# Rotary heads: scores with keys on the partitions, four heads side by side, row maxima computed beforehand

## The chip, the core and the metric

One core of a Trainium2 chip runs the whole program. The metric is the device time of one execution in microseconds; the kernel was run three times. A profile of one more execution gives every instruction's start and duration on each engine: TensorE (PE, with its weight loads as PEld), VectorE (DVE), ScalarE (ACT), GpSimd (POOL), and SyncE (SP), which issues the DMAs.

## What is computed

Two layers of an encoder, applied to a sequence of 2048 tokens and to one of 256 tokens with the same weights, D = 1024. The part that matters is in the first layer: eight rotary heads in two groups of four, each group with one key and value head of 64 channels.

```python
qa = apply_rope(rms_norm(qa.reshape(B, S, A_KV_HEADS, A_GROUPS, HEAD_DIM), qn_a), ...)
ka = apply_rope(rms_norm(ka.reshape(B, S, A_KV_HEADS, HEAD_DIM), kn_a), ...)
s_a = jnp.einsum('bqkgd,bskd->bkgqs', qa_blk, ka).astype(F32) * scale
p_a = jax.nn.softmax(s_a, axis=-1).astype(va.dtype)
o_a = jnp.einsum('bkgqs,bskd->bqkgd', p_a, va)
...
y = jnp.concatenate([o_a * jax.nn.silu(ga), o_b * jax.nn.silu(gb)], axis=-1)
return y @ w_out
```

Beside them stand four differential heads (two softmaxes each, with a distance bias), then an output projection, a gated embedding, and a second layer with a pooling mixer. All is float32. A product that needs float32 accuracy is made of parts: a value is split into a high part in TensorE's one-pass format (F32R) and the rest, and the products of the parts are added up in PSUM.

## The kernel before

Stages follow one another: norm and projections of the rotary heads (`BLOCKS` of 256 tokens, two tiles of 128 each, L265 on); attention of the rotary heads (`att_a`, L434) with the projections of the differential heads (`proj_b`, L513) as filler; attention of the differential heads (`att_b`, L603) with `proj_early` (L809: half of the output projection, the embeddings' projections, a fold of the pooling weights) as filler; then the rest of the fillers, the gate of the embedding, the pooling mixer and its output. The order within a stage is written as generators whose steps carry a nominal TensorE time. `drive` (L819) takes steps of the filler until they amount to a ratio of the main steps' time: 0.59 in `att_a` as long as `proj_b` lasts, then 0.1, and 0.34 in `att_b`. `paced` (L400) mixes the second half of one unit with the first half of the next. A scheduler then places the instructions on each engine's queue, in this order as far as their inputs are ready; each engine's queue runs in its order.

A unit of `att_a` is one tile of 128 queries, one group and one pair of heads; there are 64 with S = 2048 keys and 8 with 256. Its first half (`first`, L436, through `softmax`, L370) makes the scores of each head with the queries on the partitions: for each 512 keys two matmuls into a bank of tag `a` (L377, L378; q twice on the partitions as weights, `kA` with the high part of k in partitions 0 to 63 and the low part in the others as moving side). VectorE copies them negated into the tile `s` of 128x2048 and keeps the minimum (L442), ScalarE takes the exponential of 1024 columns at a time with the row's maximum as bias and sums the row (L389), and GpSimd inverts the sum (L448, L450) and scales `s` (L452). The second half (`second`, L457, through `chunks`, L349) transposes the probabilities on TensorE, four transposes of 128x128 for two heads and two chunks of 128 keys into a bank of tag `t` (`p_split`, L339), ScalarE copies the high part `ph` out of the bank (L343), VectorE makes the low part `pl` from the bank and `ph` (L347), and two matmuls per chunk with v as weights add to a bank of tag `o` (L470, L471; 256 columns, two heads side by side). At the end the two halves of the partitions are added (L477 to L483), GpSimd multiplies by the gate (L484) and splits the result (L121, L122), and it is stored to `yT_d`. The ends are put into `pend` and emitted among the next unit's steps. The last unit's second half (`tail`) runs beside the first unit of `att_b`.

The nine blocks of `proj_b` run twice, once for each half of the columns. One block has 96 matmuls of 256 columns (gate and v), then for each of two tiles 24 of 512 columns (q and k), a copy, a square, a sum by VectorE (L584), the inverse root by GpSimd (L109, L112), a multiplication by VectorE (L586), one by GpSimd (L587), four transposes (L591) and a split.

In `att_b` GpSimd subtracts one probability tile from another (L643). PSUM has three banks of tag `a`, three of `t`, one of `o` and one of `f` (the fillers').

## Time and profile before

| | us |
|---|---|
| median of three runs | 3475.4 (3472.97 to 3479.99) |
| span of the profiled execution | 3470.0 |
| TensorE busy | 3408.2 (98%) |
| VectorE busy | 1936.7 (56%) |
| ScalarE busy | 1671.8 (48%) |
| GpSimd busy | 1662.0 (48%) |
| share of the DMA engines, main queue | 40.4% |

The span is the time from the first to the last instruction of the execution that was profiled; the times are of other executions and include what lies around it. Busy times of TensorE count overlapping matmuls once, and their ends are modelled, so the distance between the starts of two matmuls tells more than the duration of one.

### The profile page before, as it was taken

To read this page: it belongs to the slowest core of one execution; us is meant where nothing else is said; L and a number is where in the kernel's file an instruction comes from. 1 tells how busy PE (TensorE), PEld (TensorE's weight loads), DVE (VectorE), ACT (ScalarE), POOL (GpSimd) and SP (SyncE) were. 2 spreads that over 40 slices of the span, in tenths; PEclk is the share of its full clock that TensorE was granted. 3 is DMA by queue.
4 is the path that set the end of the run, shared out by engine and by line. 5 is a ranking of instruction groups with operands and counts; after the bars stand their busy time and mean duration, and the time that the engine had idled before them with its cause. 6 is when DMAs were issued, how large, how long until landed. Compare 5 with 4: busy or idle time off the path is not lost.

```text
span 3470.0 us, 60660 instructions
## 1 busy us (share of the span) xinstructions
PE 3408.2 (98%) x21942; PEld 3043.7 (88%) x21942; DVE 1936.7 (56%) x4314; ACT 1671.8 (48%) x3108; POOL 1662.0 (48%) x2013
## 2 busy tenths in 40 slices
PE   9999999999999999999999899999999999999999
PEld 8998999998899988888888788887889999988887
DVE  4336666677666677658778787763434222342222
ACT  4235666666666666546677676751324111221111
POOL 5664545454645455337777687841113455420000
PEclk9999999999999999999999999999999999999999
DMA  7444323234423224653443525268534122353332
GB/s 250 158 141 135 112 77 109 79 109 125 141 82 98 91 77 127 190 180 108 122 125 114 149 91 149 87 196 267 186 133 157 62 72 70 99 164 115 112 113 73
DMA packets 459635, 437.76 MB, mean 126 GB/s; under 512 B 33992, under 2 KB 400584, under 8 KB 458312
## 3 DMA queue, kind: packets, MB, share of 16 engines
q1 hardware_dynamic: 459336, 433.88, 40.4%
q8 instruction: 174, 2.85, 0.3%
q14 instruction: 125, 1.02, 0.1%
HBM read 269.15 MB, written 164.63 MB: 125 GB/s over the span
## 4 chain that ended last, share of the span: by engine, by line
PE 91%; DMA 4%; DVE 2%; ACT 1%; issue 1%; POOL 0%; SPq 0%; DVEq 0%; ACTq 0%; POOLq 0%
PE pf L177 10%; PE pf L179 10%; PE pf L178 10%; PE pt L339 9%; PE pa L377 6%; PE pa L378 6%; PE po L177 6%; PE po L179 6%; PE po L178 6%; PE pa L178 4%; PE pa L177 4%; PE pa L179 4%; PE po L471 3%; PE po L470 3%; PE pt L195 2%; DMA v<-vl_d 1%
## 5 line engine op out<-in xcount | busy, mean ns | idle before, releaser
L389 ACT ACTIVATE s<-s,mx 128x1024 f32<-128x1024 f32 x512 | 585.6, 1147 | 137.3 <-DVE s L442 63.4
L347 DVE TENSOR_TENSOR pl<-pt,ph 128x512 fp32r<-128x512 f32 x780 | 522.4, 686 | 195.0 <-ACT ph L343 188.1
L343 ACT CAST ph<-pt 128x512 fp32r<-128x512 f32 x780 | 438.7, 584 | 276.3 <-PE pt L339 113.5
L339 PE MATMUL pt<-ident,s 128*128 128x128 f32 x3120 | 465.3, 273 | 4.5 <-DVE pl L347 1.9
L339 PEld LDWEIGHTS pt<-ident,s 128*128 128x128 f32 x3120 | 369.7, 141 | 52.4 <-DVE pl L347 4.6
L109 POOL TENSOR_SCALAR rstd<-ss 128x1 f32<-128x1 f32 x72 | 16.0, 222 | 656.4 <-ACT xn L184 654.8
L623 DVE CUSTOM_DVE_ANT_0 s<-pa,dist,mx 128x512 f32<-128x512 f32 x384 | 286.7, 747 | 70.5 <-PE pa L378 55.8
L643 POOL TENSOR_TENSOR s<-s 128x1024 f32<-128x1024 f32 (+1 forms) x136 | 313.0, 2318 | 0.2
L452 POOL TENSOR_SCALAR s<-s,rs 128x1024 f32<-128x1024 f32 (+1 forms) x272 | 298.6, 1110 | 12.1
L442 DVE TENSOR_SCALAR_CACHE_REDUCE s<-pa,mx 128x512 f32<-128x512 f32 x384 | 286.0, 745 | 23.2 <-PE pa L378 13.9
L470 PE MATMUL po<-ph,vA 128*128 128x256 f32 x1040 | 281.2, 292 | 1.1 <-ACT ph L343 1.1
L471 PE MATMUL po<-pl,vA 128*128 128x256 f32 x1040 | 279.5, 295 | 1.1 <-DVE pl L347 1.1
L177 PE MATMUL pf<-xh,wh 128*128 128x256 f32 x944 | 265.6, 281 | 1.7 <-DMA xh<-xTh_d 1.7
L178 PE MATMUL pf<-xl,wh 128*128 128x256 f32 x944 | 266.3, 282 | 0.5 <-DMA xl<-xTl_d 0.5
L179 PE MATMUL pf<-xh,wl 128*128 128x256 f32 x944 | 265.8, 282 | 0.7 <-DVE wl L131 0.7
L377 PE MATMUL pa<-kk,q 128*128 128x512 f32 (+1 forms) x528 | 220.8, 419 | 12.8 <-DMA kk<-kTl_d 11.5
L377 PE MATMUL pa<-kA,q 128*128 128x512 f32 (+1 forms) x528 | 222.8, 422 | 3.9 <-DVE s L442 3.7
L884 DVE TENSOR_TENSOR sg<-pp,sg 128x512 f32<-128x512 f32 x72 | 50.3, 698 | 285.3 <-ACT sg L883 280.0
L378 PE MATMUL pa<-kA,q 128*128 128x512 f32 (+1 forms) x528 | 207.0, 392 | 0.0
L378 PE MATMUL pa<-kk,q 128*128 128x512 f32 (+1 forms) x528 | 206.9, 392 | 0.0
L470 PEld LDWEIGHTS po<-ph,vA 128*128 128x128 f32 x1040 | 196.8, 189 | 11.3 <-ACT ph L343 1.7
L471 PEld LDWEIGHTS po<-pl,vA 128*128 128x128 f32 x1040 | 196.7, 189 | 7.5 <-DVE pl L347 3.0
(232 smaller groups left out, 9701.0 us busy)
## 6 DMA issues: line engine op xcount, KB each, us to landing
xr<-h_d SPq DMA_DIRECT2D x54, 512.0 KB, 3.3
q<-qTh_d SPq DMA_DIRECT2D x144, 128.0 KB, 2.9
q<-qTl_d SPq DMA_DIRECT2D x144, 128.0 KB, 3.0
xh<-xTh_d SPq DMA_DIRECT2D x18, 1024.0 KB, 5.5
xl<-xTl_d SPq DMA_DIRECT2D x18, 1024.0 KB, 7.9
h_d<-xr SPq DMA_DIRECT2D x72, 256.0 KB, 4.0
pp_d<-xr SPq DMA_DIRECT2D x72, 256.0 KB, 2.1
pp<-pp_d SPq DMA_DIRECT2D x36, 512.0 KB, 3.8
```

The source lines that it names most:

```text
L177: pe.matmul(out, lhsT=lhs[0], rhs=rhs[0], start=first, stop=False)
L178: pe.matmul(out, lhsT=lhs[0], rhs=rhs[1], start=False, stop=False)
L179: pe.matmul(out, lhsT=lhs[1], rhs=rhs[0], start=False, stop=last)
L339: pe.transpose(pt[:, (c * 2 + i) * P : (c * 2 + i + 1) * P], s[:, (c0 + c) * P : (c0 + c + 1) * P], ident)
L343: ac.copy(ph, pt)
L347: ve.tensor_tensor(out=pl, in0=pt, in1=ph.bitcast(F32), op=ALU.subtract)
L377: pe.matmul(ps, lhsT=q1, rhs=k[:, i * 512 : i * 512 + w], start=True, stop=False)
L378: pe.matmul(ps, lhsT=q2, rhs=k[:, i * 512 : i * 512 + w], start=False, stop=True)
L389: ac.activation(s[:, c], s[:, c], AF.Exp, bias=bias, scale=-1.0, accum_out=sums[i])
L470: pe.matmul(ov[0][:, 0:256], lhsT=v, rhs=ph[:, c], start=c0 + c == 0, stop=False)
L471: pe.matmul(ov[0][:, 0:256], lhsT=v, rhs=pl[:, c], start=False, stop=c0 + c == nk - 1)
L643: po.tensor_tensor(out=sc[0][:, k], in0=sc[0][:, k], in1=sc[1][:, k], op=ALU.subtract)
```

## The change

Only the rotary heads change, with what is laid out for them. A unit is now a tile of 128 queries and a whole group of four heads (32 with 2048 keys, four with 256). Three things are done in another way.

- The scores have the keys on the partitions: the weights are 128 keys, the moving side is q of four heads side by side, 512 columns. k lies in two tiles: `k1` with the high part in partitions 0 to 63 and ones in two further rows, `k2` with the low part over the high part. q lies in `q1` (high part, and two rows for the negated maximum in two parts) and `q2` (high part over low part). `load_qa` loads both and clears the two rows.
- The maximum of a row is found beforehand (`shift`): scores of the high parts alone with the queries on the partitions, 16 matmuls of 512 columns, a maximum by VectorE of each, one over all, its two parts by GpSimd, four transposes, and a copy of the two rows into `q1`. The scores then come out with the maximum taken off.
- The probabilities come out of the exponential with the keys on the partitions and are not transposed (`heads`): ScalarE takes the exponential twice, once as `ph`, once as `p`; VectorE makes `pl` = `p` - `ph`; GpSimd adds `p` to `acc`, chunk by chunk; products of 512 columns. At the end `acc` is split, a product with a selector of ones sums it over the partitions and spreads the sums, and the result is multiplied by their reciprocals.

The tiles `qr`, `kd`, `qh`, `ql` of the first stage have one buffer in place of two; the last unit of `att_a` runs ahead of `att_b`, whose first keys are loaded before, and the score tiles of `att_b` are one pool of eight.

```diff
+    def load_qa(g, tq):
+        q1 = qA.tile([P, 512], F32R, tag="q1", name="q1", bufs=2)
+        q2 = qA.tile([P, 512], F32R, tag="q2", name="q2", bufs=2)
+        po.memset(q1[64:66].bitcast(F32), 0.0)
+        for t, half, d in ((q1, 0, 0), (q2, 0, 0), (q2, 64, 1)):
+            sy.dma_start(t[half : half + 64].rearrange("p (h t) -> p h t", t=P).bitcast(F32),
+                         qT_d[d][g * 256 : g * 256 + 256, tq : tq + P].rearrange("(h d) t -> d h t", d=HD))
+        return q1, q2
...
+                k1 = k1p.tile([P, 2, T], F32R, name="k1")
+                ve.memset(k1[64:66].bitcast(F32), 1.0)
+                sy.dma_start(k1[0:64, :, 0:S0].bitcast(F32), k2[64:128, :, 0:S0].bitcast(F32))
...
-                qr = p1q.tile([P, 640], F32, tag="qr", name="qr")
+                qr = p1q.tile([P, 640], F32, tag="qr", name="qr", bufs=1)
...
+        def shift(t0, S, q):
+            n = (S + 511) // 512
+            mx = small.tile([P, 4, 4], F32, tag="mx4", name="mx4")
+            for h in range(4):
+                for i in range(n):
+                    w = min(512, S - i * 512)
+                    ps = pa()[:, :w]
+                    pe.matmul(ps, lhsT=q[0][0:66, h * P : (h + 1) * P], rhs=k1[0:66, q[2], t0 + i * 512 : t0 + i * 512 + w],
+                              start=True, stop=True)
+                    ve.tensor_reduce(out=mx[:, h, i : i + 1], in_=ps, axis=AX.X, op=ALU.max)
+                    if h * n + i < 4 * n - 1:
+                        yield
+            mn = small.tile([P, 4], F32, tag="mn", name="mn")
+            ve.tensor_reduce(out=mn, in_=mx[:, :, :n], axis=AX.X, op=ALU.max, negate=True)
+            po.tensor_scalar(out=mm[:, :, 64].bitcast(F32R), in0=mn, scalar1=1.0, scalar2=1.0, op0=ALU.mult, op1=ALU.mult)
+            po.tensor_tensor(out=mm[:, :, 65].bitcast(F32R), in0=mn, in1=mm[:, :, 64], op=ALU.subtract)
+            pt = pa()
+            for h in range(4):
+                pe.transpose(pt[0:66, h * P : (h + 1) * P], mm[:, h], ident)
+            ac.copy(q[0][64:66], pt[64:66])
...
+            def products(c, ph, pl):
+                pe.matmul(ov[0], lhsT=v, rhs=ph, start=c == 0, stop=False)
+                pe.matmul(ov[0], lhsT=v, rhs=pl, start=False, stop=c == nk - 1)
+
+            for c in range(nk):
+                ks = slice(t0 + c * P, t0 + (c + 1) * P)
+                ps = pt_()
+                pe.matmul(ps, lhsT=k1[0:66, g, ks], rhs=q[0][0:66], start=True, stop=False)
+                pe.matmul(ps, lhsT=k2[:, g, ks], rhs=q[1], start=False, stop=True)
+                ph = at.tile([P, 512], F32R, tag="ph", name="ph", bufs=4)
+                pl = at.tile([P, 512], F32R, tag="pl", name="pl", bufs=4)
+                p = at.tile([P, 512], F32, tag="p", name="p", bufs=3)
+                ac.activation(ph, ps, AF.Exp)
+                ac.activation(p, ps, AF.Exp)
+                ve.tensor_tensor(out=pl, in0=p, in1=ph.bitcast(F32), op=ALU.subtract)
+                if c == 1:
+                    po.tensor_tensor(out=acc, in0=before, in1=p, op=ALU.add)
+                elif c > 1:
+                    po.tensor_tensor(out=acc, in0=acc, in1=p, op=ALU.add)
+                before = p
...
+            split_po(acc, ah, al)
+
+            def rest1():
+                pr = pa()[:, 0:256]
+                n = 0
+                for u in range(2):
+                    for x in (ah, al):
+                        pe.matmul(pr, lhsT=sel[:, u], rhs=x[:, u * 256 : u * 256 + 256], start=n == 0, stop=n == 3)
+                        n += 1
+                rc = at.tile([P, 256], F32, tag="rc", name="rc", bufs=1)
+                ve.reciprocal(rc, pr)
+                gf = gt.rearrange("p h t -> p (h t)")
+                po.tensor_tensor(out=yt, in0=yt, in1=gf, op=ALU.mult)
+                po.tensor_tensor(out=yt, in0=yt, in1=rc, op=ALU.mult)
...
+                split_po(yt, yh, yl)
...
+                yield from paced(heads(*prev) if prev else None, shift(t0, S, q),
+                                 (n if prev is None else max(2, prev[3] // P), 4 * ((S + 511) // 512)), 19.5 * S / S0)
...
+        yield -1.0
+        for _ in heads(*prev):
+            yield 19.5 / 16
```

## Rows read from the trace of the kernel before

**Rows 1.** The page: busy us by engine (share, instructions); granted TensorE clock by slice.
```profile
PE 3408.2 (98%) x21942; PEld 3043.7 (88%) x21942; DVE 1936.7 (56%) x4314; ACT 1671.8 (48%) x3108; POOL 1662.0 (48%) x2013
...
PEclk9999999999999999999999999999999999999999
```
**Rows 2.** Busy time by stretch: length, PE, PEld, DVE, ACT, POOL, clock, DMA share.
```profile
292.00:1531.00 1239.00, 1224.51 (x8278) 1103.00 (x8277) 850.85 (x1938) 788.39 (x1444) 608.52 (x877) 1.00 0.38 113
1531.00:2290.00 759.00, 731.36 (x4621) 639.59 (x4621) 597.66 (x1509) 516.73 (x972) 581.24 (x573) 1.00 0.43 126
```
**Rows 3.** TensorE in order of time: start us, duration us, line, tiles, shape.
```profile
1104.61 0.28 PE L470 MATMUL po<-ph,vA 128*128 128x256 f32 x1
1104.73 0.28 PE L471 MATMUL po<-pl,vA 128*128 128x256 f32 x1
1104.86 1.04 PE L339 MATMUL pt<-ident,s 128*128 128x128 f32 x8
1105.65 0.48 PE L377 MATMUL pa<-kA,q 128*128 128x512 f32 x1
1105.96 0.40 PE L378 MATMUL pa<-kA,q 128*128 128x512 f32 x1
1106.20 0.40 PE L377 MATMUL pa<-kA,q 128*128 128x512 f32 x1
1106.43 0.39 PE L378 MATMUL pa<-kA,q 128*128 128x512 f32 x1
```
**Rows 4.** Groups by line, 292 to 1531 us, TensorE: count | busy us, mean ns | idle before.
```profile
L339 PE MATMUL pt<-ident,s 128*128 128x128 f32 x2084 | 307.9, 273 | 2.8 <-DVE pl L347 1.9 <-POOL s L452 0.7
L470 PE MATMUL po<-ph,vA 128*128 128x256 f32 x1040 | 281.2, 292 | 1.1 <-ACT ph L343 1.1
```
**Rows 5.** Groups by line, whole span: a ScalarE and a VectorE instruction of 512 columns.
```profile
L549 ACT ACTIVATE gs<-pf 128x512 f32<-128x512 f32 x18 | 10.8, 598 | 14.0 <-PE pf L179 13.9
...
L584 DVE TENSOR_REDUCE qss<-sq 128x8 f32<-128x512 f32 x36 | 24.5, 682 | 21.8 <-ACT sq L582 21.5
```
**Rows 6.** Groups by line, whole span, GpSimd, shapes kept apart.
```profile
L643 POOL TENSOR_TENSOR s<-s 128x1024 f32<-128x1024 f32 x128 | 307.2, 2417 | 0.0
...
L112 POOL TENSOR_TENSOR rstd<-rstd,mhalf 128x8 f32<-128x8 f32 x36 | 59.6, 1657 | 2.7
L587 POOL TENSOR_TENSOR qn<-qn,gains 128x512 f32<-128x512 f32 x36 | 46.4, 1289 | 43.5 <-DVE qn L586 31.4 <-PE pt L339 9.2 <-DMA st<-in_w_out_ab_dram 2.1
...
L122 POOL TENSOR_TENSOR yl<-mixd,yh 128x512 fp32r<-128x512 f32 x28 | 36.9, 1318 | 0.3
...
L122 POOL TENSOR_TENSOR yl<-yg,yh 128x256 fp32r<-128x256 f32 x36 | 27.3, 757 | 1.4
...
L121 POOL TENSOR_SCALAR yh<-mixd 128x512 fp32r<-128x512 f32 x28 | 18.6, 663 | 55.5 <-DVE z L1044 28.3 <-DVE z L1047 13.5 <-issue 7.2
...
L121 POOL TENSOR_SCALAR yh<-yg 128x256 fp32r<-128x256 f32 x36 | 15.6, 433 | 29.9 <-DVE yg L682 24.3 <-issue 5.4
...
L109 POOL TENSOR_SCALAR rstd<-qss 128x8 f32<-128x8 f32 x36 | 7.5, 209 | 52.6 <-DVE qss L584 51.6
```
**Rows 7.** VectorE and GpSimd in order of time, three places: start us, duration us, instruction.
```profile
693.53 1.12 POOL L452 TENSOR_SCALAR s<-s,rs 128x1024 f32<-128x1024 f32 x1
694.40 0.69 DVE L347 TENSOR_TENSOR pl<-pt,ph 128x512 fp32r<-128x512 f32 x1
...
809.50 1.67 POOL L452 TENSOR_SCALAR s<-s,rs 128x1024 f32<-128x1024 f32 x1
809.57 0.68 DVE L586 TENSOR_TENSOR qn<-qn,rstd 128x512 f32<-128x512 f32 x1
...
791.73 1.61 DVE L131 SCALAR_TENSOR_TENSOR wl<-st,gmix,wh 128x512 fp32r<-128x512 f32 x1
792.78 1.55 POOL L452 TENSOR_SCALAR s<-s,rs 128x1024 f32<-128x1024 f32 x1
```
**Rows 8.** DMA issues: count, KB each, median us to landing.
```profile
q<-qTh_d SPq DMA_DIRECT2D x144, 128.0 KB, 2.9
```

More of the change, by code (lines that the diff above doesn't have):

```diff
@@ new lines, in heads @@
+        def heads(g, tq, t0, S, q):
+            nk = S // P
+            gt = at.tile([P, 2, P], F32, tag="gt", name="gt")
+            r0 = g * 256
+            for u in range(2):
+                sy.dma_start(gt[u * 64 : u * 64 + 64],
+                             gT_d[r0 + u * P : r0 + u * P + P, tq : tq + P].rearrange("(h d) t -> d h t", d=HD))
+            ov, todo = [], []
+            acc = at.tile([P, 512], F32, tag="acc", name="acc")
+            before = None
+            def products(c, ph, pl):
@@ L466, in products @@
                 if not ov:
                     ov.append(po_())
-                for c in range(2):
-                    v = vA[:, t0 // P + c0 + c, g].rearrange("p r d -> p (r d)")
-                    pe.matmul(ov[0][:, 0:256], lhsT=v, rhs=ph[:, c], start=c0 + c == 0, stop=False)
-                    pe.matmul(ov[0][:, 0:256], lhsT=v, rhs=pl[:, c], start=False, stop=c0 + c == nk - 1)
-            yield from chunks(prs, nk, products, pend)
-            o = ov[0]
-            ot = at.tile([P, P], F32, tag="ot", name="ot", bufs=1)
@@ new lines, in heads @@
+            while pend:
+                pend.pop(0)()
+            for x in todo:
+                products(*x)
+            o = ov[0]
+            ot = at.tile([P, 256], F32, tag="ot", name="ot", bufs=1)
+            ac.copy(ot[0:64], o[64:128, 0:256])
+            ac.copy(ot[64:128], o[0:64, 256:512])
+            yt = at.tile([P, 256], F32, tag="yt", name="yt")
+            ve.tensor_tensor(out=yt[0:64], in0=o[0:64, 0:256], in1=ot[0:64], op=ALU.add)
+            ve.tensor_tensor(out=yt[64:128], in0=o[64:128, 256:512], in1=ot[64:128], op=ALU.add)
@@ L608, in att_b, with keys @@
         ac.activation(dist, dist, AF.Abs)
+        def keys(h):
+            km = []
+            for m in range(2):
+                k = kvb.tile([P, T], F32R, tag="kk", name="kk", bufs=NKK)
+                r0 = h * P + m * HD
+                for half in range(2):
+                    sy.dma_start(k[half * 64 : half * 64 + 64].bitcast(F32), kT_d[half][r0 : r0 + HD, :])
+                km.append(k)
+            return km
+        km = keys(0)
+        yield 0.0
         def first(h, t0, S, q0, km, q):
@@ L618, in first @@
                 for m in range(2):
[L619 to L620 removed]
+                    s = sB.tile([P, S0], F32, tag="s", name="s")
                     def evac(c, w, ps, before, now, s=s, off=off):
@@ L694, in att_b @@
         for h in range(4):
-            km = []
-            for m in range(2):
-                k = kvb.tile([P, T], F32R, tag="kk", name="kk", bufs=NKK)
-                r0 = h * P + m * HD
-                for half in range(2):
-                    sy.dma_start(k[half * 64 : half * 64 + 64].bitcast(F32), kT_d[half][r0 : r0 + HD, :])
-                km.append(k)
+            if h:
+                km = keys(h)
             v = None
@@ L706, in att_b @@
                     n = max(2, S // 256)
-                    got = yield from paced(second(*prev) if prev else tail[0], first(h, t0, S, q0, km, q), (n, 2 * n), 15.6 * S / S0)
-                    if prev is None:
-                        yield -1.0
+                    got = yield from paced(second(*prev) if prev else None, first(h, t0, S, q0, km, q), (n, 2 * n), 15.6 * S / S0)
                     if v is None:
@@ L908, in trunk_kernel @@
     keep.close()
-    sS_.close()
     xr = loaded(0), loaded(P)
```

120 lines of the change are left out of this document (51 added, 69 removed).

## The prediction

> **What bounds the kernel now.** I read the page first. The busy line gives TensorE (PE) 98% of the span and no other engine above 56%; the line of granted clock stands at full speed in all forty slices [rows 1]. So TensorE is the bound, and a change pays by the matmul time that it takes away, as long as TensorE is kept fed. The table by stage sharpens that: in the stretch of the rotary heads, 292 to 1531 us, TensorE is idle for 14.5 of 1239 us (98.8% busy); VectorE (DVE) is at 69%, ScalarE (ACT) at 64%, GpSimd (POOL) at 49%. In the stretch of the differential heads, where VectorE reaches 79% and GpSimd 77%, TensorE falls to 96.4% [rows 2]. The reader should keep that pair: as the helpers fill up, TensorE loses.
>
> Next the price of a matmul. Durations overlap, so I take the distance between starts in the order of time: 0.12 us for 256 columns, 0.235 for 512 (0.24 and 0.23), and for eight transposes 0.79, after which the next matmul of 512 columns needs 0.31, 0.075 more than otherwise: (0.79 + 0.075) / 8 = 0.108 a transpose [rows 3].
>
> **What TensorE gains.** The rotary heads have 36 units now (tile of 128 queries, group of four heads): 32 long ones with 2048 keys, four short ones. The groups by line show 2084 transposes in the stretch (2080 by the loops, the rest belong to the next heads) and 1040 products with the high part of p, as many as with the low [rows 4].
> - Transposes gone: 2080 x 0.108 = 224.6 us.
> - Products with v: 2080 of 256 columns become 1040 of 512: 249.6 less 244.4, 5.2 gained. Scores with keys as weights: 244.5 before and 244.4 after, nothing.
> - Maxima beforehand: 512 x 0.235 and 16 x 0.12: 122.2 added. Four transposes of the maxima and four selector products a unit: 144 x 0.108 and 144 x 0.12: 32.9 added.
> Net 75 us less, if nothing else changes. No row shows a matmul of 66 rows among matmuls of 128; it costs nothing extra, or at most the 0.075 of a change of form [rows 3] (a rival below).
>
> **What the helpers get.** ScalarE: 32 exponentials of 512 columns out of PSUM a unit, at 0.60 by the Silu of that shape [rows 5], 19.2 us; enough room. VectorE: 16 reductions for the maximum at 0.68, by the reduction of 512 columns [rows 5], and 16 subtractions p - ph. GpSimd: the row scaling goes, and instead it adds up p, chunk by chunk: 15 adds of 128x512 with two inputs. The two such instructions in the trace are 1.29 (512 columns) and 2.42 for 1024, so 1.21 [rows 6]; I take 1.25. At a unit's end come the split of the sum (0.66 and 1.32), two multiplications at 0.76, the split of the result (0.43 and 0.76) and two tiny ones at 0.21 [rows 6]: 5.1 us. With the adds 23.9 us a unit.
>
> The projections of the differential heads run as filler beside this: 18 blocks of 96 x 0.12 + 48 x 0.235 + 8 x 0.108 = 23.7 us of TensorE, and 36 tiles with 0.21 + 1.66 + 1.29 on GpSimd [rows 6]. The step costs in the code (19.5 a long unit, ratio 0.59, 22 a block) spread them over some 31 long units. One unit then needs 18.8 + 0.9 + 13.7 = 33.4 us of TensorE, and GpSimd 23.9 + 3.7 = 27.5. On that count TensorE stays the bound.
>
> **Why I don't believe that count.** The old subtraction read PSUM and one SBUF tile; the new one (p - ph) reads two SBUF tiles, and so does the work of GpSimd. The trace shows what that does. Beside a subtraction from PSUM, the scaling of 1024 columns takes GpSimd 1.12 us. Beside L586, a VectorE instruction with two SBUF inputs, the same scaling takes 1.67, 0.55 more. Where L131 (two SBUF inputs too, of the same 512 columns) and the scaling meet again and again, each waits for the other: 1.61 and 1.55 us [rows 7]. The two share a way into SBUF and use it in turn.
> The Trainium skill says it as a rule (SBUF — State Buffer, Who interferes with whom): a VectorE instruction with two SBUF inputs contends with a GpSimd instruction that reads SBUF, and the one that comes second is fully blocked until the first is done. By that rule each subtraction would cost GpSimd its whole 0.69 instead of the 0.55 of the row, 2.2 us a unit more, some 70 us more in all; I go by the row.
>
> So I sum the shared way, not the engines: 27.5 us of GpSimd a unit, 16 x 0.55 = 8.8 for the subtractions, 36 x 0.55 / 31 = 0.6 for L586: 36.9 us. TensorE's 33.4 is no longer the largest. Subtraction and add of a chunk wait for the same exponential, so they come at the same moment and meet. A way used in turn is not used without gaps; I give it the 96.4% that the bounding engine reaches in the fullest stage before [rows 2]: 38.3 us a unit.
>
> **The sum**, against the profiled execution (span 3470.0 us, the median of the three runs is 5.4 above it):
> - 75 us of matmul time gone.
> - 31 x (38.3 - 33.4) = 152 us in which TensorE waits for p and pl, now the last to arrive.
> - The 14.5 us that TensorE was idle in this stretch are inside that, so they come off.
> - The seam: the last unit used to run beside the first of the differential heads and now runs alone: ScalarE's 19.2 against 64 x 0.235 = 15.0 of TensorE, and the end of the chain (two exponentials, a subtraction): 7 us; between 0 and 15.
> - Nothing for the four short units beyond the counts above, nor for the first stage, whose tiles qr, kd, qh, ql lose a buffer: each block of two tiles has 96 x 0.12 = 11.5 us of gate products that don't touch them. Without that cover a block's second tile would wait for up to the 24 x 0.235 + 24 x 0.12 = 8.5 us of the first, 9 times. The copy of k1 is one transfer, issued before the last block's 2 x 8.5 + 11.5 us of matmuls and needed after them; it costs at most its own landing, once.
> - Nothing for the new wait of TensorE: the transposes of the maxima need a reduction (0.68, then a small one), then two tiny GpSimd instructions, and every later matmul is queued behind them on TensorE. The order before puts ready matmuls ahead of such chains (transposes waited 2.8 us in 1239) [rows 4]. With the cover gone, 0.68 + 3 x 0.21 = 1.3 us, 32 times: 42 us.
> -75 + 152 - 14.5 + 7 = +69.5: 3539.5, with the 5.4 **3545 us**. The add at 1.21 or 1.29 moves it by 19 us either way, a way without any gap (36.9 a unit) gives 3501, one used to 93% 3588: own range 3495 to 3590.
>
> **The rivals.**
> - *Subtraction and add miss each other* (the other side). VectorE has a reduction between most subtractions, and GpSimd is idle for part of a unit; if the reads fall into those gaps, TensorE stays the bound at 98.8%: 33.8 us a unit, -75 + 12 - 14.5 + 7 = -70: 3405 us. It decides at 33.4 + 82.5 / 31 = 36.1 us a unit, below which the change pays. For it: in the stage before, VectorE has 31% to spare; against it: both wait for the same event.
> - *VectorE becomes the bound*: each subtraction waits for a whole add, and the reductions stand behind it in VectorE's queue: 16 x (1.25 + 0.55 + 0.68) = 39.7, and 126 instructions of the projections at 0.68, 2.8 a unit: 42.5 us, 3675 us.
> - *q comes late*: a unit's q1 uses the buffer of the unit before the last, which is read to that one's last score; its memset on GpSimd stands behind the last adds, and the load takes 2.9 us to land [rows 8]. All of it exposed in front of the first maximum: 32 x 2.9 = 93 us on top of the first rival, 3498. Under the forecast the other waits hide it.
> - *66 rows cost a change of form*: 0.075 at 32 places for the scores and up to 32 for the maxima, 4.8 us x 32 = 154 on top of the first rival: 3559.
> The Trainium skill has a rule beside that last one (TensorEngine Tiling (Array Packing), Key Properties): changing the tiling mode drains TensorE; its modes split at 64 rows and below, so 66 would change nothing. No row here shows it either way.
>
> **How the numbers follow.** Forecast 0.60; misses 0.25, of which 0.02 end close to no change; VectorE bound 0.07; q late or form 0.08, slower both, with 0.01 within no change. A time within 0.2% of 3475.4 (3468 to 3482, about what a measurement of this kernel can tell from no change) gets 0.05 with the forecast's own lower tail; faster 0.24; slower 0.71. The range reaches into the first rival to 3425, where half of its 0.25 lies below, and up to 3605, which leaves the VectorE case out.
>
> **What would show it.** In the changed kernel the stretch of the rotary heads should take about 38 us a long unit with TensorE busy for some 85 to 90% of it; the subtraction's mean duration should stand well above 0.69 and the add's above 1.25; TensorE's waits should name ph, pl or the exponentials' banks. If the subtraction's mean is near 0.69 and TensorE near 98%, the first rival holds. If matmul starts stand further apart than 0.235 without a wait, it is the form; if the first maximum of a unit waits for a DMA, it is q. I am wrong at the root if the new subtraction doesn't take the shared way at all.

## The result and the profile after

| | before | after |
|---|---|---|
| median, us | 3477.6 | 3706.0 |
| lowest to highest | 3472.97 to 3479.99 | 3703.70 to 3708.11 |
| span of the profiled execution | 3470.0 | 3706.3 |

The ratio is 1.066, interval 1.064 to 1.067. The forecast was 3545 us with a range up to 3605: the sign was right, the loss three times as large (228 us by the medians, 236 between the two profiled executions, against 70).

The page of the changed kernel, its busy line and its line of granted clock, beside [rows 1]:

```profile
PE 3501.0 (94%) x19622; PEld 2971.1 (80%) x19622; DVE 2223.6 (60%) x3787; ACT 1647.1 (44%) x3050; POOL 2158.0 (58%) x2065
...
PEclk9997999989889989999999999999999999999999
```

TensorE is still the busiest, at 94% instead of 98%. Its busy time has grown by 93 us although it has 2320 instructions fewer, and the clock line, which was flat, now has dents. The dents explain part of the growth; how much in the middle of the rotary heads is worked out below, in the paragraph on the clock.

The table by stretch of the changed kernel; columns as in [rows 2]. The first row is the start of the rotary heads, the second their middle, the fourth the end of the differential heads.

```profile
300.00:350.00 50.00, 41.53 (x144) 29.52 (x143) 42.43 (x63) 22.29 (x42) 22.95 (x19) 0.63 0.57 166
350.00:1640.00 1290.00, 1169.78 (x5434) 915.63 (x5434) 1048.65 (x1283) 713.19 (x1293) 1044.17 (x871) 0.92 0.28 81
1640.00:1700.00 60.00, 54.21 (x234) 43.04 (x233) 42.69 (x47) 26.53 (x47) 44.10 (x36) 0.97 0.82 228
2500.00:2550.00 50.00, 37.94 (x152) 27.26 (x152) 20.64 (x34) 22.00 (x40) 2.75 (x3) 0.83 0.70 227
```

And the same stretches of the kernel before:

```profile
292.00:350.00 58.00, 52.98 (x335) 43.90 (x334) 49.73 (x108) 43.91 (x74) 28.69 (x35) 1.00 0.57 169
350.00:1480.00 1130.00, 1120.53 (x7630) 1013.86 (x7629) 769.99 (x1763) 719.87 (x1319) 562.98 (x812) 1.00 0.37 109
1480.00:1531.00 51.00, 51.00 (x319) 45.25 (x317) 31.12 (x69) 24.61 (x52) 16.85 (x31) 1.00 0.44 136
2300.00:2350.00 50.00, 47.68 (x260) 40.59 (x260) 24.09 (x40) 13.82 (x23) 7.85 (x8) 0.97 0.73 237
```

The middle is 160 us longer. No engine fills it: TensorE 91%, VectorE 81%, GpSimd 81%, ScalarE 55%. Long units start 40.9 us apart on the mean (30 distances between the instructions that close a unit's maxima), against 38.3 forecast.

The groups by line of the stretch 300 to 1697 us (count | busy us, mean ns | idle before):

```profile
L523 POOL TENSOR_TENSOR acc<-acc,p 128x512 f32<-128x512 f32 x448 | 671.9, 1500 | 112.4 <-ACT p L518 88.5 <-PE pt L935 4.8 <-PE pt L513 0.5
...
L519 DVE TENSOR_TENSOR pl<-p,ph 128x512 fp32r<-128x512 f32 x520 | 593.9, 1161 | 61.4 <-ACT p L518 43.1 <-PE po L507 13.0 <-PE po L506 1.2
L479 DVE TENSOR_REDUCE mx<-pa 128x1 f32<-128x512 f32 (+1 forms) x528 | 342.0, 670 | 112.3 <-PE pa L477 110.9
```

And TensorE's waits in the same stretch (us in total, times, longest):

```profile
PE po L507 <- DVE pl L519: 57.2, 75, 2.9
PE pa L477 <- DVE mx L479: 16.8, 20, 1.8
PE pt L512 <- ACT p L518: 15.4, 23, 1.9
PE pa L488 <- POOL mm L485: 12.0, 12, 2.4
PE pf L664 <- POOL qn L660: 10.7, 7, 3.4
```

The subtraction (L519) takes 1.16 us instead of 0.69 [rows 7], the add (L523) 1.50 instead of 1.25 to 1.29 [rows 6], and the product with `pl` is what TensorE waits for most. The maxima's reductions stand at 0.67, as costed [rows 5].

**Where the time lies.** From here on I count, in each stretch, the matmuls by width at the prices of [rows 3] (0.12, 0.235, 0.108 a transpose; 178 tiny ones left out) and call the rest of the stretch its excess: waiting, matmuls at the lower clock, and what else TensorE is counted busy beyond these prices. Over the whole execution the matmuls come to 3393.5 us before (7232 of 512 columns, 10376 of 256, 4156 transposes) and 3318.6 after (8800, 8424, 2220). That is 74.9 less, the forecast's 75. The excess went from 76.6 to 387.8, 311 more. Each row of the table is one profiled execution, with the bounds of the stretches set by that kernel's own course.

| excess, us | first stage and start | middle of the rotary heads | their end | differential heads | end of these | rest | sum |
|---|---|---|---|---|---|---|---|
| before | 16.9 | 12.6 | 0.0 | 50.4 | 4.3 | -7.6 | 76.6 |
| before, single buffers (g1_single) | 41.4 | 13.1 | 0.0 | 48.0 | 3.7 | -4.1 | 102.1 |
| changed kernel | 45.5 | 259.5 | 8.1 | 60.8 | 22.3 | -8.4 | 387.8 |
| subtractions from PSUM (e1_psum) | 43.7 | 169.4 | 5.8 | 58.8 | 16.9 | -10.7 | 283.9 |
| without adds (e2_noadd) | 43.8 | 115.9 | 9.2 | 56.1 | 21.3 | -8.8 | 237.5 |
| without subtractions (e3_nosub) | 42.1 | 105.7 | 1.7 | 52.1 | 19.3 | -9.0 | 211.9 |
| without either (f4_neither) | 41.9 | 48.6 | 19.1 | 55.7 | 21.2 | -11.2 | 175.3 |

The other rows belong to the experiments below. (The rest is below zero because its matmuls stand at 0.23 rather than 0.235.)

### The profile page after: what moved, and what is told of

It is laid out like the page before. It is cut to its first block, busy times and chain, and to the rows that moved or that the text cites. A ratio compares the mean times of both kernels' runs of the same rounds, so it can differ in the third digit from the quotient of the medians.

```text
span 3706.3 us, 54927 instructions
## 1 busy us (share of the span) xinstructions
PE 3501.0 (94%) x19622; PEld 2971.1 (80%) x19622; DVE 2223.6 (60%) x3787; ACT 1647.1 (44%) x3050; POOL 2158.0 (58%) x2065
## 3 DMA queue, kind: packets, MB, share of 16 engines
q1 hardware_dynamic: 449688, 430.21, 38.3%
## 4 chain that ended last, share of the span: by engine, by line
PE 76%; DVE 8%; DMA 5%; POOL 5%; issue 3%; ACT 2%; SPq 0%; POOLq 0%; DVEq 0%; ACTq 0%
PE pf L178 9%; PE pf L179 9%; PE pf L180 9%; PE po L178 6%; PE po L180 6%; PE po L179 6%; PE pa L178 4%; PE pa L179 4%; PE pa L180 4%; DVE pl L519 3%; PE pa L409 3%; PE pa L410 3%; PE pt L371 3%; DVE mx L479 3%; POOL acc L523 2%
## 5 line engine op out<-in xcount | busy, mean ns | idle before, releaser
L523 POOL TENSOR_TENSOR acc<-acc,p 128x512 f32<-128x512 f32 x448 | 671.9, 1500 | 112.4 <-ACT p L518 88.5
L519 DVE TENSOR_TENSOR pl<-p,ph 128x512 fp32r<-128x512 f32 x520 | 593.9, 1161 | 61.4 <-ACT p L518 43.1
L479 DVE TENSOR_REDUCE mx<-pa 128x1 f32<-128x512 f32 (+1 forms) x528 | 342.0, 670 | 112.3 <-PE pa L477 110.9
L517 ACT ACTIVATE ph<-pt 128x512 fp32r<-128x512 f32 x520 | 312.9, 605 | 179.5 <-PE pt L513 132.8
L518 ACT ACTIVATE p<-pt 128x512 f32<-128x512 f32 x520 | 313.1, 605 | 115.5 <-POOL acc L523 68.2
L421 ACT ACTIVATE s<-s,mx 128x1024 f32<-128x1024 f32 x256 | 292.7, 1147 | 88.3 <-DVE mx L708 86.6
L507 PE MATMUL po<-pl,vA 128*128 128x512 f32 x520 | 233.1, 448 | 58.6 <-DVE pl L519 57.2
L477 PE MATMUL pa<-k,q 66*128 66x512 f32 (+1 forms) x528 | 222.7, 453 | 25.4 <-DVE mx L479 16.8
L512 PE MATMUL pt<-q,k 66*128 66x512 f32 x520 | 225.5, 434 | 16.9 <-ACT p L518 15.4
L513 PE MATMUL pt<-q,k 128*128 128x512 f32 x520 | 219.6, 422 | 0.0
```

The lines of the kernel that those rows point to most:

```text
L479: ve.tensor_reduce(out=mx[:, h, i : i + 1], in_=ps, axis=AX.X, op=ALU.max)
L507: pe.matmul(ov[0], lhsT=v, rhs=pl, start=False, stop=c == nk - 1)
L517: ac.activation(ph, ps, AF.Exp)
L518: ac.activation(p, ps, AF.Exp)
L519: ve.tensor_tensor(out=pl, in0=p, in1=ph.bitcast(F32), op=ALU.subtract)
L523: po.tensor_tensor(out=acc, in0=acc, in1=p, op=ALU.add)
```

## The experiments

The theory after the result: subtraction and add meet on the shared way, as forecast, TensorE waits, and its clock falls, which the sum left out. Rivals: the order of TensorE's queue (maxima, seams between units) makes the waits whatever the helpers take; or the helpers' load does it without any sharing. All times are medians, to be held against 3473 to 3478 for the kernel before and 3706.0 for the changed one.

**Take the meeting away.** The second exponential is written over the scores in PSUM, so that the subtraction has one SBUF input.

```diff
-                ac.activation(p, ps, AF.Exp)
-                ve.tensor_tensor(out=pl, in0=p, in1=ph.bitcast(F32), op=ALU.subtract)
+                ac.activation(ps, ps, AF.Exp)
+                ve.tensor_tensor(out=pl, in0=ps, in1=ph.bitcast(F32), op=ALU.subtract)
...
-                    po.tensor_tensor(out=acc, in0=acc, in1=p, op=ALU.add)
+                    po.tensor_tensor(out=acc, in0=acc, in1=ph.bitcast(F32), op=ALU.add)
```

> The second exponential is written over the scores in PSUM instead of into an SBUF tile, so the subtraction reads PSUM and one SBUF tile, as the kernel before did; GpSimd adds up the high parts alone (the row sums leave out the low parts). Instruction counts on every engine stay. Theory (the two-input subtraction and GpSimd's add use one way in turn; TensorE waits, and its clock falls to the lower level): the subtraction goes back from 1.16 to about 0.69 us, the add from 1.50 to about 1.27, TensorE is busy for 97% or more of the stretch of the rotary heads at a granted clock of 0.99 or more, and the time is 3400 to 3460 us. Rival (the order of TensorE's queue: transposes of the maxima and products that wait at the head of it, whatever the helpers' instructions take): the waits stay, 3620 us or more. Second rival (GpSimd's own 27 us a unit come too late even without sharing): the add goes back to 1.27 but TensorE still waits, 3550 to 3620.

Measured: 3613.4 us, ratio 1.041 (1.038 to 1.043). The groups by line, 300 to 1697 us, and then the busy time of the middle:

```profile
L522 POOL TENSOR_TENSOR acc<-acc,ph 128x512 f32<-128x512 f32 x448 | 587.1, 1311 | 205.0 <-ACT ph L516 184.2 <-PE pt L513 3.9 <-PE pf L180 0.2
L518 DVE TENSOR_TENSOR pl<-pt,ph 128x512 fp32r<-128x512 f32 x520 | 350.0, 681 | 142.1 <-ACT pt L517 136.8 <-PE pt L513 3.8
```
```profile
350.00:1550.00 1200.00, 1123.29 (x5431) 894.65 (x5429) 822.88 (x1281) 705.71 (x1290) 888.03 (x871) 0.95 0.31 88
```

Both durations fell to what they are alone (all 520 subtractions under 0.70 us), and 93 us came back. So the meeting is real and costs 93 us. (The variant also holds the scores' bank until the subtraction; where there are no adds, that made no difference, 3560 against 3556 us below.) But the kernel stays 140 us above the one before, with TensorE at a clock of 0.95 in the middle, and the theory had asked for 3400 to 3460. The time lies in the range of the second rival (3550 to 3620: the add is back at its own duration, and TensorE waits all the same). The next runs ask whether it is GpSimd's load alone, as that rival says.

**Take the work away.** The first run leaves out fourteen of the fifteen adds of a unit (the one left reads one tile), the second leaves out the subtraction and uses the high part twice, the third leaves out both.

```diff
 e2_noadd
-                    po.tensor_tensor(out=acc, in0=before, in1=p, op=ALU.add)
-                elif c > 1:
-                    po.tensor_tensor(out=acc, in0=acc, in1=p, op=ALU.add)
+                    po.tensor_scalar(out=acc, in0=before, scalar1=1.0, scalar2=1.0, op0=ALU.mult, op1=ALU.add)
 e3_nosub
-                ve.tensor_tensor(out=pl, in0=p, in1=ph.bitcast(F32), op=ALU.subtract)
...
-                todo.append((c, ph, pl))
+                todo.append((c, ph, ph))
```

> Of the fifteen adds of a unit one is left (it reads one tile and adds a constant), so the row sums are left out of the computation; everything else stays, the two-input subtraction too. Theory: with nothing of GpSimd's beside it the subtraction is near 0.7 us and the time is 3400 to 3460 us, as where the subtraction reads PSUM. Rival (the order of TensorE's queue): 3620 us or more. Rival (the two reads of SBUF are slow by themselves, without GpSimd): the subtraction stays above 1.0 us.

> The subtraction is left out and the products read the high part twice (the low part of the probabilities is left out of the computation); both exponentials and all adds stay. Theory (sharing): the adds go to about 1.27 us, GpSimd needs 27.5 us a unit against TensorE's 33.4, and the time is 3400 to 3460 us. Rival (GpSimd's adds by themselves are the bound, the subtraction only waits along): the adds alone hold the unit, 3550 us or more.

> Both the subtractions and fourteen of fifteen adds are left out (the low parts of the probabilities and the row sums are left out of the computation), so nothing is left that could meet on the shared way within a unit. Without the subtraction alone the time was 3533 us, without the adds alone 3556. Theory A (what is left there is the helpers' load): now 3400 to 3460 us. Theory B (what is left is the seam between two units: the last products, the transposes of the maxima, the load of q and the first maxima stand one behind the other on TensorE with little ready work between them): 3490 to 3530 us, with the waits and low clock still at the seam.

Measured: 3556.4, 3533.4 and 3495.9 us (the last 1.006, 1.005 to 1.008). The first two meet none of the times that were expected: sharing alone (3400 to 3460) would have been faster, the rivals (3620 or 3550 and more) slower. The subtraction without adds, the add without subtractions, and the middle with neither:

```profile
L519 DVE TENSOR_TENSOR pl<-p,ph 128x512 fp32r<-128x512 f32 x520 | 390.0, 767 | 76.0 <-ACT p L518 59.5 <-PE po L507 15.0 <-PE pt L513 0.4
```
```profile
L521 POOL TENSOR_TENSOR acc<-acc,p 128x512 f32<-128x512 f32 x448 | 584.7, 1305 | 137.8 <-ACT p L517 117.0 <-DVE mn L483 2.5 <-DMA q<-qTh_d 1.5
```
```profile
350.00:1400.00 1050.00, 1016.34 (x5304) 854.47 (x5304) 489.23 (x753) 669.00 (x1244) 313.20 (x435) 0.99 0.33 95
...
2300.00:2350.00 50.00, 39.31 (x128) 27.23 (x127) 15.05 (x24) 14.79 (x26) 1.13 (x2) 0.74 0.71 228
```

This gives a ladder. With neither, the kernel is 23 us above the one before although 75 us of matmuls are gone. The adds alone cost 37 us more, the subtractions alone 60, both kept apart 117 (e1_psum), both together 210. So GpSimd's load, the second rival of e1_psum, is only a part of it. By the table, the steps lie in the middle stretch: 49, 106, 116, 169, 260. With neither, that stretch runs at a clock of 0.99, and most of what is left sits at the edges of the stages. Theory B of the last expectation was right in size (3490 to 3530) and largely wrong in place: the seams between units are in the middle stretch, whose excess is only 36 us above before; 63 us more lie in the other columns of the table.

**Is the subtraction's cost its two inputs?**

> The subtraction reads PSUM and one SBUF tile, and fourteen of fifteen adds are left out (row sums left out of the computation), so VectorE has its load and GpSimd next to none. With neither subtraction nor adds 3496 us, with the two-input subtraction alone 3556. If it is VectorE's load (16 x 0.68 us more a unit, and its place between scores and products) that cost the 60 us: 3540 to 3560 us. If it is the second SBUF input, slow or held up even without the adds: 3500 to 3520 us.

The edit is e1_psum and e2_noadd together. Measured: 3560.2 us (1.025, 1.023 to 1.026), the same as with two SBUF inputs (3556.4). So the second input is free in time where GpSimd has no adds to make, and 60 us are the price of the subtraction itself, by VectorE's load or by its place between scores and products; the run can't tell these two apart.

**Are the adds waited for as a whole?** Each add as two of 256 columns.

```diff
+                    for x in (slice(0, 256), slice(256, 512)):
+                        po.tensor_tensor(out=acc[:, x], in0=acc[:, x], in1=p[:, x], op=ALU.add)
```

> The changed kernel with every add done as two of 256 columns, one after the other (each about 0.72 us by the multiplications of that size, so 0.18 us more a chunk for GpSimd). If a subtraction that comes second waits for the whole instruction of GpSimd: its longest durations fall from 1.7 to 1.8 us to about 1.4 (0.69 + 0.72), its mean from 1.16 to 0.95 to 1.05, and the time to 3640 to 3700 us in spite of the longer adds. If the two share the way evenly while both run: mean and longest stay, and the time rises to 3710 to 3760 us.

Measured: 3728.5 us (1.072).

```profile
L525 POOL TENSOR_TENSOR acc<-acc,p 128x256 f32<-128x256 f32 x869 | 769.6, 912 | 55.9 <-ACT p L518 52.2
L519 DVE TENSOR_TENSOR pl<-p,ph 128x512 fp32r<-128x512 f32 x506 | 473.2, 945 | 129.6 <-ACT p L518 117.4 <-PE po L507 4.1 <-PE pf L180 1.3
```

In the changed kernel 180 of 520 subtractions took 1.35 us or more (up to 1.83) and 179 under 0.8; with halved adds 10 and 209, and the mean fell to 0.95. So a subtraction that comes second waits for the end of GpSimd's instruction, as the first answer says; the ten that are left are up to 1.80 us. But the time rose, into the range of the second answer: a chunk now costs GpSimd 2 x 0.91 = 1.82 us instead of 1.50. What shorter waits on VectorE gave was lost on GpSimd; the run doesn't say what they would be worth alone.

**Is the low clock a cause of its own?** The first score matmul of each chunk is done twice.

```diff
+                pe.matmul(ps, lhsT=k1[0:66, g, ks], rhs=q[0][0:66], start=True, stop=True)
```

> Nothing is left out; the first score matmul of every chunk is done twice, the second time over the first, which adds 16 x 0.235 = 3.8 us of TensorE work to a long unit, 122 us in all, just where TensorE is idle between chunks. Three answers. If the lower clock is what was missing in my sum (busy time 184 us above what the same matmuls take at full clock, idle 133 us as forecast), the added work keeps the clock up and the time falls or hardly rises: 3560 to 3690 us, granted clock in the stretch above 0.96. If VectorE and GpSimd set the pace at 41 us a unit and the clock only follows, nothing changes: 3690 to 3730. If TensorE is the bound at its lower clock, the added work comes on top: 3800 us or more, clock about 0.91.

Measured: 3729.2 us (1.073). 520 matmuls, 122 us at 0.235, cost 23 us. The middle stretch:

```profile
350.00:1670.00 1320.00, 1232.64 (x5923) 994.41 (x5922) 1042.00 (x1283) 724.11 (x1291) 1044.39 (x869) 0.95 0.28 81
```

In the changed kernel TensorE was idle there for 120 of 1290 us, and busy for 139 us more than its matmuls' price. Here it is idle for 87 and over price by 87 (1232.6 less 1145.2). The added work took the place of both. So in this stretch the helpers set the pace, and the second answer holds in size (3690 to 3730), though not to the letter: it said that nothing changes, and the time rose by 23 us.

**Do the maxima and the seams cost more than their matmuls?** Two runs leave out the maxima with all that belongs to them: f3_nomax starts from the changed kernel, h1_bare from the variant with neither subtractions nor adds. g3_seam, from that variant too, keeps the maxima and has a third buffer of q1, the two small instructions of the maxima on VectorE, and products three chunks behind the scores.

```diff
 f3_nomax, h1_bare
-                    pe.matmul(ps, lhsT=q[0][0:66, h * P : (h + 1) * P], rhs=k1[0:66, q[2], t0 + i * 512 : t0 + i * 512 + w],
-                              start=True, stop=True)
-                    ve.tensor_reduce(out=mx[:, h, i : i + 1], in_=ps, axis=AX.X, op=ALU.max)
...
-                ac.activation(ph, ps, AF.Exp)
+                ac.activation(ph, ps, AF.Exp, scale=0.01)
 g3_seam
-LATE_A = 2
+LATE_A = 3
...
-        q1 = qA.tile([P, 512], F32R, tag="q1", name="q1", bufs=2)
+        q1 = qA.tile([P, 512], F32R, tag="q1", name="q1", bufs=3)
...
-            po.tensor_tensor(out=mm[:, :, 65].bitcast(F32R), in0=mn, in1=mm[:, :, 64], op=ALU.subtract)
+            ve.tensor_tensor(out=mm[:, :, 65].bitcast(F32R), in0=mn, in1=mm[:, :, 64], op=ALU.subtract)
```

> The maxima are left out, with their matmuls, reductions, transposes and the copy into q (the scores are scaled down by 0.01 in the exponentials instead, so that they stay finite); subtractions and adds stay as in the changed kernel. The matmuls that go are 138 us. If the maxima cost their matmul time alone: 3568 us. If the pace is set by the shared way (36.9 us a unit, whatever the maxima do): about 3545 to 3600. If the chain of the maxima and VectorE's 16 reductions between the subtractions are what makes TensorE wait beyond my sum: 3430 to 3520.

> Subtractions, adds and the maxima with all that belongs to them are left out together (scores scaled down by 0.01 in the exponentials). Without subtractions and adds alone it was 3496 us. The matmuls of the maxima are 138 us. If the maxima cost only these: 3350 to 3365 us. If the waits that are left (20 us where the first unit's maxima run alone, 36 us at the seams) belong to the chain of the maxima: 3300 to 3335 us. If the seam costs the same without them, because products and scores of two units follow each other there: above 3350.

> The variant without subtractions and adds (3496 us; low parts and row sums left out of the computation) with the three repairs of the seam between two units: a third buffer of q1, the two small instructions of the maxima on VectorE, products three chunks behind the scores. There TensorE loses 36 us at the 32 seams, beside 44 us at the start, the ends and the first stage that these repairs don't touch. If the chain of the maxima and the load of q make the seam: 3460 to 3480 us. If it is the order of the queue whatever stands in it: 3485 to 3500.

Measured: 3585.6, 3352.5 and 3495.7 us. Without maxima, subtractions and adds the time is 143 us below that without the last two: the 138 us of matmuls and no chain worth naming. In the changed kernel even a little less came back, 120, which fits the answer that the middle's pace isn't TensorE's there (3545 to 3600). The seam's repairs gave nothing once the helpers were out of the way (3495.7 against 3495.9).

**Repairs where the helpers work.** On e1_psum: q1's third buffer (f1_q3); products three chunks behind (g2_late); the small instructions of the maxima on VectorE (i1_mm); all three (f2_all). The last but one also on the changed kernel itself (i2_mm). The edits are those of g3_seam.

> On top of the variant with the exponential in PSUM (3613 us): q1 gets a third buffer, so the load of a unit's q no longer waits for the last score of the unit before the last. If the load is part of the seam: 3570 to 3600 us, and no wait of a maximum for q is left. If the other waits of the seam cover it: 3605 to 3620.

> The variant with the exponential in PSUM (3613 us), and the products three chunks behind the scores instead of two; q and the two small instructions of the maxima as in the changed kernel. With these two changed as well it was 3573 us, with q alone 3609. If the closeness of product and subtraction is what helped: 3570 to 3585 us, and the products' wait for the subtraction falls from 25 us to under 12. If it was the maxima's way round GpSimd: 3600 us or more.

> The variant with the exponential in PSUM (3613 us) with one further change: the two small instructions of the maxima on VectorE instead of GpSimd. With q1's third buffer alone it was 3609, with later products alone 3603, with all three 3573. If the maxima's way round GpSimd is what the three-part variant gained: 3575 to 3590 us, and the transposes wait less than the 10.1 us of that variant. If the three only work together (each alone moves the wait to the next): 3600 to 3615.

> On top of that: the two small instructions of the maxima on VectorE instead of GpSimd (there they stand behind an add), and the products one chunk later (three chunks behind the scores instead of two, with five buffers of the two parts). If the seam's chain and the closeness of product and subtraction hold what is left (waits of products for the subtraction 45 us, of the transposes 13, of first maxima 44, and the low clock behind them): 3480 to 3560 us. If it is the load of VectorE: 3590 us or more.

> The changed kernel itself (3706 us) with the two small instructions of the maxima on VectorE instead of GpSimd. The transposes of the maxima waited 12.0 us for GpSimd there. If that wait and the low clock behind it are an own term: 3670 to 3695 us. If the meeting of subtraction and add sets the pace in the middle of the stretch, whatever the maxima wait for: 3698 to 3715.

Measured: 3608.5, 3603.4, 3588.0, 3573.1 (1.028, 1.027 to 1.030), and 3700.0. Against 3613.4 the first is 5 us (within the scatter of the two), the second 10, the third 25, all three 40: by the medians they add up. All three stay above the 3480 to 3560 us that were expected if the seam and the closeness of product and subtraction held all that was left. Moving the maxima's two instructions out of GpSimd's queue is the largest single gain; on the changed kernel it is worth 6 us, hardly more than the scatter, as expected if the meeting sets the pace there. How the 25 us come about isn't shown: the transposes' own wait fell only from 10.1 to 6.9 us (300 to 1600 us). How TensorE's waits move (300 to 1600 us), e1_psum first, then g2_late:

```profile
PE po L507 <- DVE pl L518: 25.4, 36, 2.3
...
PE pt L512 <- DVE pl L518: 5.5, 5, 1.9
```
```profile
PE pt L512 <- DVE pl L518: 16.4, 23, 2.7
PE po L507 <- DVE pl L518: 11.8, 12, 1.8
```

Later products wait less for the subtraction, but the next scores wait more for it, since it holds their bank. None of these variants reaches the kernel before.

**The single buffers.** The kernel before with `bufs=1` for `qr`, `kd`, `qh` and `ql`, and nothing else.

```diff
-                qr = p1q.tile([P, 640], F32, tag="qr", name="qr")
+                qr = p1q.tile([P, 640], F32, tag="qr", name="qr", bufs=1)
```

> The kernel before with one buffer instead of two for the four tiles of the first stage, and nothing else of the change. The changed kernel's first stage ends 8 to 11 us later and TensorE waits there 8.0 us, four times, for VectorE's qn, which holds the banks of the projections. If the single buffers are that: 8 to 13 us slower than before, a ratio of about 1.003. If it is the work placed beside the last block (the copy of k1, the memsets, the first loads): within 3 us.

Measured: 3494.7 us, ratio 1.0046 (1.0034 to 1.0059), 16 us, more than the 8 to 13 expected. TensorE's waits, 0 to 320 us:

```profile
PE pa L177 <- DVE qn L290: 8.0, 4, 2.9
PE pa L377 <- DVE qn L290: 5.4, 1, 5.4
```

The first row is the changed kernel's own, where the same wait is 8.0 us in four. The second comes at the start of the heads, which my expectation left out. In the table the first stage and the start have the same excess here (41.4) as in every variant of the changed kernel there (41.9 to 45.5).

## Why the prediction missed, by its steps

| term | forecast | profiled executions |
|---|---|---|
| matmuls | -75 | -74.9 |
| middle of the rotary heads (+152, -14.5) | +137.5 | +246.9 |
| seam behind the last unit | +7 | +8.1 |
| first stage and start | 0 | +28.6 |
| differential heads and their end | 0 | +28.4 |
| rest | 0 | -0.8 |
| sum | +69.5 | +236.3 |

**The matmul count held.** So did the price of nothing for matmuls of 66 rows: among those of 128 they stand 0.23 apart (the variant without subtractions, in order of time), which takes the rival of the change of form away:

```profile
735.16 0.39 PE L512 MATMUL pt<-q,k 66*128 66x512 f32 x1
735.39 0.40 PE L513 MATMUL pt<-q,k 128*128 128x512 f32 x1
735.62 0.40 PE L512 MATMUL pt<-q,k 66*128 66x512 f32 x1
```

The late q is no term either: 2.3 us of waits in the changed kernel's stretch name it, and a third buffer gave 5 on e1_psum, within the scatter. The transposes of the maxima, put at nothing because ready matmuls would cover them, waited 12.0 us in twelve places in the changed kernel; taking their two small instructions away from GpSimd gave 6 us there.

**The shared way was rightly seen and mis-priced.** Its signs all appeared: a subtraction at 1.16, adds at 1.50, waits for `pl`, TensorE 91% busy in the middle (85 to 90 had been expected). Four microseconds of the changed kernel, in order of time:

```profile
1305.07 1.54 DVE L519 TENSOR_TENSOR pl<-p,ph 128x512 fp32r<-128x512 f32 x1
1306.03 1.72 POOL L523 TENSOR_TENSOR acc<-acc,p 128x512 f32<-128x512 f32 x1
1307.14 1.17 DVE L519 TENSOR_TENSOR pl<-p,ph 128x512 fp32r<-128x512 f32 x1
1308.83 0.67 DVE L519 TENSOR_TENSOR pl<-p,ph 128x512 fp32r<-128x512 f32 x1
```

Both sides pay. I charged 0.55 us to GpSimd for each subtraction and nothing to VectorE; measured, the add pays 0.19 on the mean (1.50 less 1.31) and the subtraction 0.48 (1.16 less 0.68). The meeting's price, the step from e1_psum to the changed kernel, is 93 us.
Counted over the changed kernel, 72 adds began with 0.4 to 0.6 us (0.51 on the mean) of a subtraction left and met no other; they took 0.34 longer than 1.31. Ten subtractions began in the same way with more than 1 us (1.22 on the mean) of an add left; they took 1.09 longer than 0.68. So the second loses what is left of the first, less some 0.15 us. An add does not lose the whole 0.69 of a subtraction, only what is left of it when the add begins.
The rule of the Trainium skill that I had weighed (SBUF — State Buffer, Who interferes with whom: the one that comes second is fully blocked until the first is done) would have put some 70 us more on the sum, 3615. The trace agrees with the lock (the instructions just counted); the 70 us came of charging the whole subtraction each time.

**The step that failed is the rule that I summed by**: that the pace of a stretch is that of its fullest resource (36.9 us a unit of the shared way against 33.4 of TensorE), and that all else hides behind it. The shared way was not full: in the middle of the changed kernel, GpSimd or a VectorE instruction with two SBUF inputs (L519, L659) runs during 1093 of 1290 us, 85% where the sum had 96.4%. TensorE lost time at every lower load too. With subtraction and add kept apart, VectorE is 69% and GpSimd 74% busy in the middle (e1_psum), hardly more for VectorE than before (68%), and TensorE still loses 169 us there. The subtractions alone bring 60 us, the adds alone 37, which a maximum over the resources puts at nothing. Of the 246.9 us of the middle, the table gives 90 to the meeting (259.5 less 169.4) and 157 to what stays with both kept apart (169.4 less 12.6). My first rival made the same mistake in the other direction: it gave 3405 us where the reads miss each other, and kept apart by construction they gave 3613. So the sign of the forecast was right in part by luck: by its own sum the change would have paid without the meeting, and without the meeting it still loses 140 us.
Why such a load went with 12.6 us of excess before and with 169 now is settled only in part. A chunk now goes through scores, two exponentials, subtraction and product within two chunks of TensorE's queue, and a queue in fixed order passes each delay of a helper on: that is argued. Shown is that three changes of buffers, engine and order gave 40 of the 117 us back. What the rest is made of stays open.

**The clock was missing from the sum; in the middle it is no term of its own.** There the granted clock fell to 0.92. One place, the busy time in steps of 5 us, and then TensorE in order of time:

```profile
1295.00:1300.00 5.00, 4.60 (x22) 3.51 (x20) 4.92 (x8) 4.30 (x10) 4.75 (x6) 1.00 0.02 4
1300.00:1305.00 5.00, 3.52 (x9) 1.77 (x10) 5.00 (x6) 1.91 (x4) 5.00 (x5) 0.81 0.09 27
1305.00:1310.00 5.00, 5.00 (x15) 3.83 (x15) 5.00 (x7) 2.96 (x7) 5.00 (x4) 0.50 0.13 26
1310.00:1315.00 5.00, 5.00 (x23) 4.10 (x22) 5.00 (x8) 3.34 (x7) 4.76 (x4) 1.00 0.51 131
```
```profile
1305.20 0.63 PE L506 MATMUL po<-ph,vA 128*128 128x512 f32 x1
1305.62 0.63 PE L477 MATMUL pa<-k,q 66*128 66x512 f32 x1
1306.05 0.63 PE L512 MATMUL pt<-q,k 66*128 66x512 f32 x1
```

TensorE is idle for 1.5 of 5 us, then runs at the lower level (0.50, that is 1.2 of 2.4 GHz) with starts 0.43 apart, then comes back. In the middle, 198 us lie at the lower level. Of the 259.5 us of excess 103.0 fall into them (19.5 idle) and 156.5 into time at the full clock: 100.6 idle, and 55.9 counted busy beyond the prices. But in e4_twice the added matmuls came out of the idle and the slow time (136.5 us at the lower level), and the end didn't come earlier. So less slow time alone bought nothing in this stretch; for the others no run tells.

**Costed at nothing: the single buffers.** The excess of the first stage and the start grew by 28.6 us; single buffers alone make 24.5 of it between the profiled executions, which lie 25.7 us apart, and 16 us of the whole time by the medians. I had found 11.5 us of gate products that hide each block, and named the price without that cover, up to 8.5 us in nine places. The cover held but for four waits of 2 us; at the start of the heads, behind the last block, there was none, and I had not looked there.

**Not in the sum at all: the differential heads**, 28.4 us, 18 of it at their end. TensorE waits there for ScalarE's and VectorE's preparation of the fillers' operands, at a clock of 0.83 (waits of TensorE in the changed kernel, 2440 to 2570 us):

```profile
PE pf L846 <- ACT xr L857: 4.0, 3, 2.6
PE pa L178 <- ACT whi L128: 2.8, 1, 2.8
PE pf L178 <- ACT xr L857: 2.5, 3, 1.2
PE pf L178 <- DVE pq L119: 2.1, 3, 0.9
```

The end's excess is there in every variant of the changed kernel in the table (16.9 to 22.3) and not with single buffers alone (3.7); no run tried it. That the fillers stand in another place since the last rotary unit runs ahead is only argued. For the other 10 us, in the heads themselves, no run gives a cause.

The rival "VectorE becomes the bound" came nearest by its number (3675), which is luck, as its mechanism isn't there: it had each subtraction at 1.80 us and VectorE full; measured, the mean is 1.16, a third of the subtractions wait for half of an add or more, a third don't wait, and VectorE is 81% busy.

## What to carry to other kernels

A bound summed per engine, or per shared way, left out here what TensorE loses while nothing is full: 169 us of a stretch of 1200 with VectorE at 69% and GpSimd at 74%, where the kernel before lost 12.6 of 1130 with VectorE at 68% and GpSimd at 50%. So put a price on each helper's instruction that a product waits for, and take it from a run that leaves the instruction out. Price a shared resource on both sides of it, and read the price from the step between "together" and "apart". And a buffer taken away at the far end of a stage is a term of its own: here 16 us, a fifth of the whole gain in matmuls.

## What the runs showed of the hardware that was not expected

- A VectorE subtraction with two SBUF inputs takes as long as one from PSUM (median 0.68 us in e2_noadd and h2_dve; 3556 and 3560 us) when GpSimd has no adds to make; its mean is then 0.77, and beside an add it takes up to 1.83 us.
- Where subtraction and add meet, the one that comes second loses what is left of the first less some 0.15 us (0.34 of 0.51 us for 72 adds, 1.09 of 1.22 for ten subtractions).
- The reciprocal of 128x256 out of PSUM takes 1.75 us, four times an addition of that width on 64 partitions (0.41 to 0.43); it stands in VectorE's queue once a unit and had no price in the sum. Group by line, 300 to 1697 us, of the changed kernel:

```profile
L555 DVE RECIPROCAL rc<-pa 128x256 f32<-128x256 f32 x36 | 62.9, 1748 | 6.0 <-PE pa L552 6.0
...
L541 DVE TENSOR_TENSOR yt<-po,ot 64x256 f32<-64x256 f32 x36 | 14.7, 409 | 15.7 <-ACT ot L539 10.3 <-POOL yl L123 4.4 <-POOL al L123 0.6
```

- 122 us of TensorE work added between waits cost 23 us, and the granted clock of the middle rose from 0.92 to 0.95.
